# A two-layer backbone on one core: layer 0's first projection unit by quarters, and a re-ordered expert route before its mixture of experts

## The chip, the core and the metric

The kernel runs on one core of one Trainium2 chip. Its time is the device time of one execution in microseconds. The core's engines are TensorE (PE, matrix products), VectorE (DVE), ScalarE (ACT), GpSimd (POOL) and SyncE (SP, which here issues nearly all loads). Each engine works through its own instructions in order; one engine waits for another, or for a transfer, by semaphores.

## What is computed

Two layers over 256 latent tokens and, in layer 0, also 256 context tokens of width 1024, all in fp32. Layer 0's mixer is a gated recurrence (RG-LRU) beside a gated linear attention (GLA), layer 1's is a grouped-query attention. Each is followed by a mixture of 16 experts in 4 groups, of which every token takes two experts of one group. Cut to what matters here:

```python
def adaln(cvec, w, b):                       # shift, scale and gate of both sub-layers
    m = jax.nn.silu(cvec) @ w + b
    return tuple(m.reshape(m.shape[0], 6, 1, D_MODEL)[:, j] for j in range(6))

hl = modulate(rmsnorm(xl, norm1[i]), sh1l, sc1l)      # h * (1 + scale) + shift, per column
hc = modulate(rmsnorm(xc, norm1[i]), sh1c, sc1c)
# layer 0: project(h) = split(h @ w_in), its first 512 columns are xa; u = dwconv(xa)
xl = xl + g1l * yl
hl2 = modulate(rmsnorm(xl, norm2[i]), sh2l, sc2l)

def hier_moe(h, wg, bg, we, be, w1, w3, w2):
    p_group = softmax(t @ wg + bg);  w_group, g_idx = top_k(p_group, 1)
    e_val, e_idx = top_k(logits of the experts in that group, 2)
    w_exp = softmax(e_val) * w_group
    for e in range(16):
        he = silu(t @ w1[e]) * (t @ w3[e])
        out = out + comb[:, e:e + 1] * (he @ w2[e])
```

## The kernel before

**Weights.** About 305 MB come from HBM through one queue, SP's, in a fixed list (`order`, with `plan`). `feed(key)` hands out the next weight tile and lets `pump` issue loads as far ahead as there are slots; a slot is a 1 MB tile `raw`, and a load into it waits until the last reader of what lay there is done. `less_slots` and `more_slots` take slots out and put them in. Where full precision is wanted, a weight half (128x1024) is split by `split` (L534) into `whi`, a rounded copy made on ACT, and `wlo`, the rest, made on DVE or POOL; the moved operand is split in the same way (`hhi`, `hlo`, or `xh`, `xl`), and `mm3` (L557) adds three products hi·lo, hi·hi and lo·hi.

**Order.** A scheduler places most instructions by their dependences and priorities. `pin(where)` (L156) switches single engines to the order of the program, by the table `PIN`: letters a, d, g, p, s for ACT, DVE, POOL, PE and SP.

**The first unit** (layer 0). The norm's scale and shift come from a product of the conditioning vector with `w_ada`. For the first norm it is made in four parts: `ad0(n, h)` (L448) loads 4 chunks of 256 KB for each half of part n, multiplies them, and `ad0_cols` (L460) copies the result (ACT, `ad`), turns it on PE, and makes columns `A` (scale) and `B` (shift) of two 128-blocks of channels on DVE. `norm_T` (L620) turns the normed input to `xw` (channels on partitions); `finish(n)` scales and shifts two of its eight blocks (4 DVE instructions of 128x256) and splits them into `hhi` (ACT) and `hlo` (DVE). `first_unit` (L680) multiplies by the first 512 columns of `w_in`: 8 blocks x 4 column groups x 3 products = 96 matmuls into four accumulators, block after block; a table `AD0` says after which of its 16 steps the next `ad0` half or `finish` is written. `LO_U0` puts its four `wlo` on POOL. Of the other loads, `mod[0]` (0.25 MB) comes ahead of these weights, `bd` and `mod[1]` behind the third part. The `lam` instructions are a chain of some twenty tiny DVE instructions on the recurrence's parameters, free to fall between.

**From there to the route** PE works through the other units of `w_in`, the recurrence, the linear attention and `w_out`.

**Layer 0's route** (L798 to L1060). For each of four token tiles, `choose` (L813) takes the two best experts from the logits, with masks `Mb`, `Mf` and per choice `M`. `tile_` (L885) writes the normed tokens `h2x` to DRAM; for the last tile it does so on ACT and POOL (`on_pool`). `route_end` (L920) finds each token's place within its expert by a product of `Mb` with a triangle `tri`, ranks the experts by their counts (`units`, L967), and sorts them into 12 units: the four largest experts have a unit each, and the others share one by two. `prepare` and `tables` (L1010, L1045) make one-hot matrices `oh` of the places and multiply them with the tokens' numbers: the lists `t0i`, by which POOL's indirect DMAs gather each unit's tokens `xg` from DRAM. `prep_x` (L1570) turns and splits these (`xh`, `xl`), and `hidden(i, n, h)` (L1614) multiplies them with half h of weight n of unit i. Which expert a unit has is read from `order` by SP (L1545) before its loads can be issued. At L1666 all engines read a count and at L1667 branch around a block for tokens beyond their expert's room. Three loads are issued ahead of this branch, on slots opened by `more_slots` with a small POOL copy each (`state["behind"]`).

**The rest** is layer 0's experts, layer 1's attention, its route (with a branch at L2174) and its experts in 8 pairs.

Nearly every instruction goes through one helper, L144, so the profile's groups are told apart by tile names.

## Time and profile before

| | |
|---|---|
| three runs | 1022.48, 1022.91, 1026.24 us, median 1022.91 |
| the profiled execution | 1020.54 us, span from first to last instruction 1018.8 us |
| granted TensorE clock, mean | 0.956 of full |
| busy, share of the span | PE 90%, DVE 52%, ACT 39%, POOL 16% |
| moved by DMA | 304.56 MB, 299 GB/s in the mean |

The stages in the profiled execution, in us from its start: 0 to 72 the first unit, to 300 the rest of the mixer, 300 to 345 the route with the branch, to about 580 the steady part of layer 0's experts, to about 640 their end, to 780 layer 1's attention, to 800 its route, and to 1019 its experts. The mean busy shares hide these differences, so the windows by stage are read first, then the timeline inside the two stages that the change touches. PE's busy time counts a matmul from its start to a modelled end, and two in a row overlap; the distance from one start to the next is the better measure.

### The profile page before, as it was taken

To read this page: it belongs to the slowest core of one execution; us is meant where nothing else is said; L and a number is where in the kernel's file an instruction comes from. 1 tells how busy PE (TensorE), PEld (TensorE's weight loads), DVE (VectorE), ACT (ScalarE), POOL (GpSimd) and SP (SyncE) were. 2 spreads that over 40 slices of the span, in tenths; PEclk is the share of its full clock that TensorE was granted. 3 is DMA by queue.
4 is the path that set the end of the run, shared out by engine and by line. 5 is a ranking of instruction groups with operands and counts; after the bars stand their busy time and mean duration, and the time that the engine had idled before them with its cause. 6 is when DMAs were issued, how large, how long until landed. Compare 5 with 4: busy or idle time off the path is not lost. (4 is left out here: it accounts for less than half of the span.)

```text
span 1018.8 us, 12604 instructions
## 1 busy us (share of the span) xinstructions
PE 913.9 (90%) x4549; PEld 535.3 (53%) x4549; DVE 534.8 (52%) x1039; ACT 396.2 (39%) x687; POOL 162.5 (16%) x163
## 2 busy tenths in 40 slices
PE   5899997999991899989999966998996899999997
PEld 3456465667761555647466433774575444443432
DVE  5458578538587565636456347878657111111112
ACT  3236745144231544637455423453545222121210
POOL 2103332040503400001100233023001000000000
PEclk9899999999995899999999978999998999999999
DMA  9925454559541899999999976845928699999993
GB/s 315 384 100 218 155 198 172 206 182 336 197 160 49 307 419 421 421 420 403 408 422 400 380 306 248 302 171 200 369 95 307 234 419 417 416 418 414 417 414 136
DMA packets 63165, 304.56 MB, mean 299 GB/s; under 512 B 8578, under 2 KB 17666, under 8 KB 35056
## 3 DMA queue, kind: packets, MB, share of 16 engines
q1 hardware_dynamic: 55216, 284.56, 71.4%
q0 software_dynamic: 5120, 14.06, 3.7%
q10 hardware_dynamic: 2752, 4.98, 1.3%
q8 instruction: 40, 0.66, 0.3%
q14 instruction: 37, 0.30, 0.1%
HBM read 294.76 MB, written 12.58 MB: 302 GB/s over the span
## 5 line engine op out<-in xcount | busy, mean ns | idle before, releaser
L144 DVE TENSOR_TENSOR wlo<-raw,whi 128x1024 fp32r<-128x1024 f32 x138 | 170.4, 1250 | 77.4 <-ACT whi L144 70.2
L144 ACT ACTIVATE whi<-raw 128x1024 fp32r<-128x1024 f32 x140 | 146.4, 1057 | 119.4 <-PE acc L144 100.4
L144 PE MATMUL aux<-raw,x 128*64 128x512 f32 x488 | 116.3, 597 | 2.0 <-PEq L2174 1.4
L144 PEld LDWEIGHTS aux<-raw,x 128*64 128x64 f32 x488 | 34.5, 136 | 62.9 <-issue 58.6
L144 PE MATMUL acc<-raw,xf 128*64 128x512 f32 x256 | 62.3, 598 | 2.2 <-DMA raw<-in_w_dram 2.2
L144 PE MATMUL aux<-raw,sl 128*64 128x512 f32 x240 | 58.7, 610 | 0.7 <-ACT sl L144 0.7
L144 PE MATMUL acc<-wlo,xh 128*128 128x512 f32 x128 | 52.1, 407 | 6.4 <-DVE wlo L144 3.6
L144 PE MATMUL ada<-raw,cT 128*32 128x512 f32 x320 | 54.7, 616 | 1.0 <-DMA raw<-in_w_ada_dram 1.0
L144 PE MATMUL acc<-whi,xh 128*128 128x512 f32 x128 | 53.5, 418 | 0.0
L144 PE MATMUL acc<-whi,xl 128*128 128x512 f32 x128 | 51.8, 405 | 0.0
L144 PE MATMUL acc<-raw,hf 128*64 128x512 f32 x128 | 38.6, 659 | 7.9 <-DMA raw<-in_w_dram 7.8
L144 DVE SCALAR_TENSOR_TENSOR aux<-aux,ws,mod 128x512 f32<-128x512 f32 x8 | 6.1, 760 | 73.3 <-PE aux L144 73.3
L144 PE MATMUL acc<-hhi,whi 128*128 128x512 f32 x96 | 38.5, 417 | 6.2 <-ACT hhi L144 6.2
L144 POOL DMA_INDIRECT yd<-y,t0i x10 | 11.7, 1173 | 191.6 <-ACT y L144 156.5
L144 PE MATMUL acc<-whi,h 128*128 128x512 f32 x128 | 41.7, 400 | 0.0
L144 PEld LDWEIGHTS acc<-raw,xf 128*64 128x64 f32 x256 | 19.1, 136 | 38.4 <-issue 30.9
L144 PE MATMUL acc<-hlo,whi 128*128 128x512 f32 x96 | 38.9, 406 | 0.2 <-DVE hlo L144 0.2
L144 PE MATMUL acc<-hhi,wlo 128*128 128x512 f32 x96 | 39.0, 406 | 0.0
L144 DVE TENSOR_TENSOR he<-sl,aux 128x512 f32<-128x512 f32 x8 | 8.4, 1056 | 56.2 <-PE aux L144 56.2
L144 PEld LDWEIGHTS aux<-raw,sl 128*64 128x64 f32 x240 | 18.2, 140 | 37.1 <-issue 35.0
L144 PEld LDWEIGHTS acc<-wlo,xh 128*128 128x128 f32 x128 | 25.1, 196 | 12.3 <-DVE wlo L144 4.0
L144 PEld LDWEIGHTS acc<-whi,xh 128*128 128x128 f32 x128 | 25.0, 195 | 10.1 <-issue 3.5
(444 smaller groups left out, 1850.5 us busy)
## 6 DMA issues: line engine op xcount, KB each, us to landing
raw<-in_w_dram SPq DMA_DIRECT2D x151, 1024.0 KB, 15.0
raw<-in_w_ada_dram SPq DMA_DIRECT2D x38, 1024.0 KB, 6.3
raw<-in_w_dram SPq DMA_DIRECT2D x72, 512.0 KB, 11.5
raw<-in_w_in_dram SPq DMA_DIRECT2D x10, 1024.0 KB, 5.1
raw<-in_w_ada_dram SPq DMA_DIRECT2D x32, 256.0 KB, 6.9
raw<-in_w_qkv_dram SPq DMA_DIRECT2D x6, 1024.0 KB, 12.8
xres<-in_w_dram SPq DMA_DIRECT2D x5, 1024.0 KB
raw<-in_w_out_dram SPq DMA_DIRECT2D x4, 1024.0 KB, 7.5
```

What stands on the lines that cost most here:

```text
L144: ins = f(*a, **k)
```

## The change

**The first unit.** It is written as a pipeline over four quarters of two blocks each: 8 products hi·hi, then the next part's `ad0` with its copy, 8 products with `hlo`, the turn of the copy and the columns, 8 products with `wlo`, then the next part's scaling and splitting. Program order is kept on PE, ACT and DVE throughout. The four `wlo` are on DVE. The `lam` chain is ahead of the norm. The loads of `mod[0]` and `mod[1]` come together with `bd` behind the third quarter; `pcol` and the input come first.

**Layer 0's route.** The last tile's `h2x` is made on DVE, with its second half behind the choice (`early`). The masks per choice (`MM`) are made tile by tile in `choose`. `to_units` makes the eight one-hot matrices in two DVE instructions and one PE batch; the order of the experts (`experts`), the weights, counts (`others`, `weights_of`) and the hold list come behind the gathers. The first two gathers write into one tile, `xg01`, that ACT zeroes early. One load is issued ahead of the branch, and the branch stands ahead of `prep_x(0)` and all weight splits of unit 0; the slots of `parts_p` are opened behind `prep_x(1)`, without POOL's copies. Layer 1's route takes the shorter `weights` too.

```diff
-PIN = dict(pair='p', px='g', m0='p')
+PIN = dict(pair='p', px='padg', re='da', tb='dag', m0='p', n1='pad', xa='pad')
-LO_U0 = '1111'
@@ loads
-    sp.dma_start(mod[0], I["bada"][0])
...
-            if n == 3:
-                sp.dma_start(bd, I["bd"])
-                sp.dma_start(mod[1], I["bada"][1])
@@ first_unit
-        for n in range(4):
-            if n % 2 == 0:
-                raw = feed(("w_in", 0, n // 2))
-            state["lo"] = pool if LO_U0[n] == "1" else dve
-            wh, wl = split(raw[:, n % 2 * 1024:(n % 2 + 1) * 1024])
...
-                    mm3(pss[m], w, (hh[:, k, :], hl[:, k, :]), k == 0, k == KD - 1)
...
-                while at and at[0] == 4 * n + m:
-                    at.pop(0)
-                    todo.pop(0)()
+        copy, turn, rest = columns(0)
+        copy()
+        turn_last()
+        turn()
+        scaled(6)
+        rest()
+        x, hi = weights_hi(0)
+        modulate(0)
+        w = hi, weights_lo(x, hi)
+        scaled(7)
+        for n in range(3):
+            products(n, 0, w)
+            for h in range(2):
+                ad0(n + 1, h)
+            copy, turn, rest = columns(n + 1)
+            copy()
+            x, hi = weights_hi(n + 1)
+            products(n, 1, w)
+            turn()
+            rest()
+            products(n, 2, w)
+            modulate(n + 1)
+            w = hi, weights_lo(x, hi)
+        sp.dma_start(bd, I["bd"])
+        for l in range(2):
+            sp.dma_start(mod[l], I["bada"][l])
+        for m in range(4):
+            for kk in range(2):
+                for j in range(3):
+                    product(3, m, kk, j, w)
+            done(m, pss[m])
@@ tile_
-                if on_pool:
-                    act.activation(a, x[:, n * 512:(n + 1) * 512], AF.Copy, scale=rss[t])
-                    pool.tensor_tensor(a, a, A2[i][n], op=ALU.mult)
...
+                if late and n:
+                    todo.append(shift)
                 else:
...
+                    shift()
@@ to_units (new)
+            def one_hot(k):
+                sl = slice(k * NT, (k + 1) * NT)
+                dve.tensor_tensor(oh[:, sl, :], iota.unsqueeze(1).to_broadcast([P, NT, P]),
+                                  pk[:, sl].unsqueeze(2).to_broadcast([P, NT, P]), op=ALU.is_equal)
...
+            for n in range(NK):
+                pe.matmul(ps[:, 0:2 * NU], oh[:, n, :], v[:, n, 0:2, :].rearrange("p a u -> p (a u)"),
+                          start=(n == 0), stop=(n == NK - 1))
@@ from the gathers to the first expert
+    xg01 = parts_p.tile([P, 2048], F32, tag="raw", name="xg01")
+    act.activation(xg01.rearrange("p (n s) -> p n s", s=P), iota.unsqueeze(1).to_broadcast([P, 16, P]), AF.Copy, scale=0.0)
...
+    for e in range(2):
+        fetch_x(e)
+    R.experts()
...
+    state["behind"] = None
+    pump(state["fed"] + 1 + len(slots))
+    more_slots(raw2_p, N_RAW2 - R_ST - R_YB)
+    R.others()
+    wgt = weights_of()
...
-    pin("px")
-    for e in range(2):
-        with high_if(FH):
-            fetch_x(e)
-    xgs0 = xgs[0]
-    prep_x(0)
-    prep_x(1)
-
-    state["behind"] = (wgt[:, 0:1], xgs0[:, 0:1], xs[0][0][:, 0, 0:1].bitcast(F32), ident[:, 0:1])[BEH]
-    more_slots(raw2_p, N_RAW2 - R_ST - R_YB)
-    more_slots(parts_p, N_PARTS)
     rv = nc.values_load(R.cnt[0:1, 0:1], min_val=0, max_val=NTOK)
     with tc.If(rv > 0):
...
+    pin("px")
+    prep_x(0)
+    pin("tb")
+    ahead()
+    pin("px")
+    prep_x(1)
+    more_slots(parts_p, N_PARTS)
     pin("m0")
     hidden(0, 0, 0)
```

How this moves instructions, at four places. PE in the first unit, from the turn of part 0 on, before (`ad` is a part of the norm's product, `acc` the unit's accumulators):

```order
L144 MATMUL aux<-ident,ad_307 128x128 x4
L144 MATMUL ad_343<-raw,cT 32x512 x3
L144 MATMUL acc<-hhi,whi 128x512 x3
L144 MATMUL ad_343<-raw,cT 32x512
L144 MATMUL acc<-hlo,whi 128x512
L144 MATMUL acc<-hhi,wlo 128x512
```

The same place after:

```order
L136 MATMUL aux<-ident,ad_301 128x128 x4
L136 MATMUL acc<-hhi,whi 128x512 x8
L136 MATMUL ad_340<-raw,cT 32x512 x8
L136 MATMUL acc<-hlo,whi 128x512 x8
L136 MATMUL aux<-ident,ad_349 128x128 x4
L136 MATMUL acc<-hhi,wlo 128x512 x8
```

The first quarter's 8 products hi·hi stand ahead of the next part's product, and that part's copy is turned before the quarter's last 8 products; before, part 1 was turned after all 24. On DVE, the last part and the unit's end, before:

```order
L144 TENSOR_REDUCE v_472<-aux 128x8
L144 TENSOR_TENSOR A_0_136<-v_472,n1c 128x4
L144 TENSOR_TENSOR B_0_137<-v_472,b1c 128x4
L144 TENSOR_TENSOR A_0_136<-A_0_136,bn 128x4
L144 TENSOR_SCALAR xw<-xw,A_0_136,B_0_137 128x256 x4
L144 TENSOR_TENSOR hlo<-xw,hhi 128x512
L144 TENSOR_TENSOR wlo<-raw,whi 128x1024 x2
```

and after:

```order
L136 TENSOR_REDUCE v_475<-aux 128x8
L136 TENSOR_TENSOR A_0_173<-v_475,n1c 128x4
L136 TENSOR_TENSOR B_0_174<-v_475,b1c 128x4
L136 TENSOR_TENSOR A_0_173<-A_0_173,bn 128x4
L136 TENSOR_SCALAR xw<-xw,A_0_173,B_0_174 128x256 x4
L136 TENSOR_TENSOR hlo<-xw,hhi 128x512 x2
L136 TENSOR_TENSOR wlo<-raw,whi 128x1024 x3
```

The first of the three `wlo` is now the quarter's own, which was POOL's; the other two belong to the next unit in both. On POOL, the end of the route before (`h2x` is the last tile, `xg` the gathered tokens, L1666 the count):

```order
L144 TENSOR_TENSOR xa_2424<-xa_2424,row 128x512
L144 TENSOR_TENSOR h2x<-xa_2424,row 128x64x8
L144 TENSOR_TENSOR xa_2428<-xa_2428,row 128x512
L144 TENSOR_TENSOR h2x<-xa_2428,row 128x64x8
L144 MEMSET xg 128x1024
L144 COPY raw<-ident 128x1
L144 DMA xg<-h2d_112,t0i 128x1024
L144 MEMSET xg 128x1024
L144 DMA xg<-h2d_112,t0i 128x1024
L144 COPY raw<-ident 128x1 x3
L1666 TENSOR_LOAD cnti
```

and after:

```order
L136 TENSOR_TENSOR r_2222<-ssq,half_neg 128x1
L136 TENSOR_TENSOR r_2305<-ssq,half_neg 128x1
L136 TENSOR_TENSOR r_2386<-ssq,half_neg 128x1
L136 DMA xg_2528<-h2d_113,ix 128x1024 x2
L1781 TENSOR_LOAD cnti
```

Nothing but the two gathers is left of it. On ACT, around the branch before (L1666 and L1667):

```order
L144 ACTIVATE whi<-raw 128x1024 x2
L144 ACTIVATE m_2473<-m_2473 128x4
L144 ACTIVATE whi<-raw 128x1024 x2
L144 ACTIVATE xh<-aux 128x512 x2
L144 ACTIVATE xf<-aux 128x512 x2
L144 ACTIVATE whi<-raw 128x1024 x2
L1666 TENSOR_LOAD cnti
L1667 COMPARE_AND_BRANCH
```

and after, behind the branch's end:

```order
L1782 UNCONDITIONAL_BRANCH
L136 ACT_TABLE_LOAD
L136 ACTIVATE xh<-aux 128x512 x2
L136 ACTIVATE whi<-raw 128x1024 x4
L136 ACTIVATE xf<-aux 128x512 x2
L136 ACTIVATE whi<-raw 128x1024 x4
```

All eight copies `whi` of unit 0, of which six stood ahead of the branch, now follow it.

## Rows read from the trace of the kernel before

**Rows 1.** Windows by stage: length, busy per engine (instructions), TensorE clock, DMA share, GB/s.

```profile
80.00:300.00 220.00, 210.27 (x1297) 138.46 (x1295) 151.84 (x254) 96.58 (x162) 60.94 (x62) 0.99 0.56 202
...
320.00:345.00 25.00, 13.19 (x52) 10.90 (x53) 10.21 (x38) 6.03 (x8) 4.11 (x7) 0.64 0.45 165
346.00:580.00 234.00, 227.44 (x1004) 137.79 (x1004) 129.13 (x142) 126.63 (x155) 31.31 (x34) 0.99 1.00 408
```

**Rows 2.** Timeline, first unit: start, length, engine, line, operation, count, idle before and releaser.

```profile
17.90 0.60 ACT L144 ACTIVATE ad<-ad 128x512 f32<-128x512 f32 x1 [2.27 <-PE ad L144]
...
20.49 4.65 POOL L144 TENSOR_TENSOR wlo<-raw,whi 128x1024 fp32r<-128x1024 f32 x2 [7.30 <-ACT whi L144]
20.60 2.27 DVE L144 TENSOR_SCALAR lam<-lam 128x8 f32<-128x8 f32 x1
...
27.03 1.22 PE L144 MATMUL acc<-hhi,whi 128*128 128x512 f32 x2 [4.34 <-ACT hhi L144]
```

**Rows 3.** SP timeline, part 3 issued; DMA view of 20 to 60 us, median landing.

```profile
26.88 7.78 SPq L144 DMA_DIRECT2D raw<-in_w_ada_dram  x8
...
raw<-in_w_ada_dram SPq DMA_DIRECT2D x16, 256.0 KB, 7.3
```

**Rows 4.** Windows inside the first unit, columns as in the first group.

```profile
30.00:33.00 3.00, 3.00 (x7) 2.07 (x7) 0.00 (x0) 0.00 (x0) 0.00 (x0) 0.51 1.04 402
33.00:36.00 3.00, 3.00 (x14) 2.46 (x14) 0.00 (x0) 0.00 (x0) 0.00 (x0) 1.00 1.07 348
...
50.00:52.00 2.00, 0.57 (x2) 0.25 (x2) 1.95 (x6) 1.26 (x2) 0.00 (x0) 1.00 0.73 240
```

**Rows 5.** Timeline, second part, and the end of the first unit.

```profile
36.61 1.06 PE L144 MATMUL ad<-raw,cT 128*32 128x512 f32 x8
...
37.82 0.60 ACT L144 ACTIVATE ad<-ad 128x512 f32<-128x512 f32 x1 [10.05 <-PE ad L144]
...
38.48 0.66 PE L144 MATMUL aux<-ident,ad 128*128 128x128 f32 x4 [0.80 <-ACT ad L144]
...
39.79 1.38 DVE L144 TENSOR_SCALAR xw<-xw,A,B 128x256 f32<-128x256 f32 x4
...
40.56 1.28 ACT L144 ACTIVATE hhi<-xw 128x512 fp32r<-128x512 f32 x2 [2.14 <-DVE xw L144]
...
63.31 2.36 DVE L144 TENSOR_TENSOR wlo<-raw,whi 128x1024 fp32r<-128x1024 f32 x2 [0.26 <-ACT whi L144]
...
68.02 2.06 ACT L144 ACTIVATE xa<-acc 128x512 f32<-128x512 f32 x4 [3.27 <-PE acc L144]
```

**Rows 6.** Timeline, the route from the last tile to the first transposed tokens.

```profile
306.38 1.32 POOL L144 TENSOR_TENSOR h2x<-xa,row 128x512 f32<-128x512 f32 x1
...
306.49 1.31 DVE L144 TENSOR_TENSOR gt<-lg 128x80 f32<-128x80 f32 x1
...
319.22 1.22 DVE L144 TENSOR_TENSOR wlo<-raw,whi 128x1024 fp32r<-128x1024 f32 x1
...
323.57 3.70 PE L144 MATMUL aux<-vals,oh 128*128 128x36 f32 x14 [1.12 <-DVE vals L144]
...
328.79 1.25 POOL L144 DMA_INDIRECT xg<-h2d,t0i  x1 [8.31 <-DVE t0i L144]
...
333.39 1.94 PE L144 MATMUL aux<-ident,xg 128*128 128x128 f32 x8 [6.11 <-DMA xg<-h2d,t0i]
```

**Rows 7.** Timeline around layer 0's branch, then PE behind layer 1's.

```profile
343.50 0.70 PE L144 MATMUL acc<-wlo,xh 128*128 128x512 f32 x1 [2.77 <-PEq L1667]
...
345.40 8.76 SPq L144 DMA_DIRECT2D raw<-in_w_dram  x4
...
352.25 0.39 PE L144 MATMUL acc<-whi,xl 128*128 128x512 f32 x1
...
796.45 3.65 PE L144 MATMUL aux<-raw,x 128*64 128x512 f32 x16 [1.36 <-PEq L2174]
```

**Rows 8.** Window behind layer 0's branch, columns as in the first group.

```profile
342.00:346.00 4.00, 2.50 (x6) 2.07 (x7) 1.23 (x1) 1.56 (x2) 0.73 (x1) 0.70 0.18 68
```

358 lines of the change are left out of this document (208 added, 150 removed).

## The prediction

> **What bounds the kernel now.** I read the windows by stage first [rows 1]. From 80 to 300 us PE is busy 210.3 of 220 us at a clock of 0.99: PE sets the pace there, and whatever comes before moves the whole stretch with it. From 346 to 580 us PE is busy 227.4 of 234 us while the DMA share is 1.00: the loads set the pace, closely followed by PE. Between them, from 320 to 345 us, PE is busy 13.2 of 25 us at a clock of 0.64 and DMA 0.45: a chain of waits, and nothing is the bound by its size. The first 72 us are another such chain.
>
> In the first unit, the timeline shows why [rows 2]. Part 0's copy `ad` is at 17.90, yet the first product starts at 27.03, after PE had waited 4.34 us for `hhi`. In between POOL makes two `wlo` (4.65 us), and a `lam` instruction of 128x8 elements on DVE takes 2.27 us beside it. The second part shows the undisturbed length [rows 5]: copy at 37.82, turn at 38.48, scaling from 39.79, `hhi` from 40.56, which ends for its first block at about 41.2. That is 3.4 us against 9.1. The copies `xa` that end the unit start at 68.02, so it is over at about 69. Its last inputs had come long before: the last chunk of part 3 is issued at 34.7 and the median landing is 7.3 us later, so 42 [rows 3]. From 42 to 69 the unit works off what it could have done while the loads came.
>
> **The first unit, after.** A quarter's chain, in the order of PE's program, with lengths from [rows 4, 5]. Fourteen matmuls fit in 3.00 us at full clock, so one takes 0.22 us, against seven, 0.43 us, at half clock.
> - 8 products hi·hi: 1.8.
> - 16 matmuls of the next part (two batches of 8 at 1.06): 2.1.
> - 8 products with `hlo`: 1.8; the copy (0.60) lies beside them.
> - turn 0.66, columns about 0.7 (from the turn's end to 39.79), one block's scaling 0.7 (half of 1.38), one `hhi` 0.64 (half of 1.28).
>
> This is 8.4 us; the 8 products with `wlo` (1.8) lie beside the columns and the scaling. The quarter's own `wlo` on DVE (half of 2.36, so 1.2) comes after the scaling and is wanted two batches later, so it is hidden, except in the last quarter.
>
> The first quarter starts at 17.9 + 3.4 = 21.3; 0.7 us earlier, since 0.25 MB (`mod[0]`) at 348 GB/s are no longer ahead of it; and up to 1.5 us later, since three blocks' turns and scalings by row stand ahead of the columns on DVE. I take 22.0. Three chains lead to 22.0 + 25.2 = 47.2. The last quarter multiplies column group by column group and wants `wlo` at once: that is there after the second `hhi`, an `hlo` (half as wide as a split: estimated 0.7) and the split, 0.6 + 0.7 + 1.2, at 49.7; some 22 products remain, 4.8, and a few of the next work's matmuls, 0.5. The end is 55, against 69: **14 us less**. The loads allow it: part 3 lands at about 41.3, and the third quarter wants it at 22.0 + 16.8 + 1.8 = 40.6, under one us of wait. `bd` and `mod`, now behind the third quarter, find the queue empty.
>
> The bounds: 15 if the start is at 21.3; 11 if the first quarter's PE work (6.4 us in the chain) runs mostly at half clock. Behind it the stretch to 300 us has the same order of instructions on every engine, apart from a few `hf` and `u` on DVE, so the 14 us pass through; DVE is busy only 152 of 220 us there [rows 1].
>
> **Layer 0's route, up to the gathers.** Three covers go away. POOL's work on the last tile: while it makes `h2x` (1.32), a small comparison on DVE takes 1.31 [rows 6]; four such POOL instructions lie beside the choice of the last tile, and I take 2 us for them. Three `wlo` stand in the chain of the lists on DVE, 1.22 each: 3.7. The one-hot products take 3.70 us for the last 14 matmuls of 16; eight remain, about 2, so 1.7 less, but the two large one-hot instructions and the masks per tile cost some of it. Together 7 us: the first gather starts at about 322 in the time of before, not at 328.8.
>
> **And behind them.** Here most of it is given back. Ahead of the first product now stand eight weight matmuls and the branch on PE, and behind the branch ACT makes the table load, `xh`, and all eight `whi`, each followed by its `wlo`. My estimate is that the tokens and the counts are there near 327, and that the weight matmuls, at half clock, bring PE to the branch at about 331.5. The branch kept PE idle for 2.77 us in layer 0, and in layer 1, with little DMA traffic, for 1.36 [rows 7]; I take 2.8, so 334.3. Then the turns of the first half of the tokens (1 of 1.94 at half clock, [rows 6]), two `xh` (I estimate 0.6 each, as for `hhi`), and a `whi` of about 1.1 and a `wlo` of 1.22 with what lies between: the first product is at about 338.4, some 3 us later than before. No branch interrupts it now, but eight `wlo` at 1.22 take 9.8 us, and the first products run at half clock: unit 0's 48 products end at 351 to 352.5. In the kernel before the last of them starts at 352.25 [rows 7]. So for PE the gain is nil to 1 us.
>
> For the stage that follows, the loads count [rows 1]. Before, 3 MB were issued ahead of the branch, and behind it DMA moved 68 GB/s for 4 us, [rows 8]; the next load is issued at 345.40 [rows 7]. After, only 1 MB is issued ahead of it: 2 MB less, some 5 us at 408 GB/s. Against that, loads resume near 333, as slots come free by the splits, and three gathers of 0.5 MB each, which ran between the loads, now run while the queue is short: 3.7 us. The 4 us of near silence are gone for the greater part. I take **2 us less** in all, with bounds of 7 less (the whole lead is kept) and 4 more (the slots come free so late that the missing 2 MB are paid and little else is gained).
>
> A rule of the Trainium skill bears on the price of the branch. Runtime: NRT & Kernel Launch, Instruction fetch mechanics, says that a taken branch out of the fetched window forces a DMA fetch of the target before the engine can go on. The two branches agree with it, 2.77 against 1.36 us of idle PE with and without loads in the queues. By it the branch after, with 1 MB queued and not 3, would be nearer to 1.4, and the sum 1 us lower.
>
> **Layer 1's route** computes its weights with fewer instructions, but PE is busy with its gather products up to the branch: 0, within 0.5 either way.
>
> **The sum.** The profiled execution took 1020.5 us (span 1018.8), 2.4 below the median of the three runs, 1022.9. From the median: 1022.9 - 14 - 2 = **1006.9**.
>
> **Rivals.**
> - *The route keeps its lead.* If slots come free as fast as the splits run, the loads stand 7 us earlier, and PE follows. That gives 1022.9 - 14 - 7 = 1002, and 1000 with the better bound of the first unit. For it speaks that the silence behind the branch shrinks; against it, that all of unit 0's splits stand behind the branch. Chance 0.20.
> - *The early loads do not do what they say.* One load is ahead of the branch where there were three. If unit 0's last slots come free only near 347, and the two new slots of `parts_p` wait behind them in SP's order, the stream is 4 us later: 1022.9 - 14 + 4 = 1013. Chance 0.17.
> - *The first unit is bound by DVE or waits, not by the chain above.* The splits and columns are all on one engine now, in program order; if each quarter loses 2 us by that, or one quarter runs at half clock (see below), only half of the 14 is won: 1022.9 - 7 - 2 = 1014, up to 1017. Chance 0.09.
> - *Slower: the clock stays down in the first unit.* PE's clock fell to one half after it had waited 4.34 us ahead of its first product, and came back within some 6 us of work [rows 2, 4]; in the window from 50 to 52 us, with PE busy 0.57 of 2 us, it stayed at full. The pipeline has waits of 1 to 2 us before every quarter. If the clock were at one half throughout, a quarter would cost 24 x 0.43 + 16 x 0.26 + 1.3 for the turn = 15.8 and not 8.4, four of them 63: the end at 22 + 63 = 85, 16 us later than now, and the time 1022.9 + 16 - 2 = 1037. Two such quarters use up the 14 us, and from three on the kernel is slower. The row from 50 to 52 speaks against it. Chance 0.03.
>
> The skill has a rule that points that way: TensorE: Matmul & The Clock Gate, Part 1, calls the throttled state the default, which activity releases. By it alone a unit cut into short batches with waits would run at half clock, and the time would be the 1037 of the last rival; the row from 50 to 52 us, full clock across such a wait, does not bear this out.
>
> **How the numbers follow.** The sum as forecast, 0.51. Its own bounds are 1022.9 - 15 - 4 = 1004 and 1022.9 - 12 - 0 = 1011. The range goes to 999 at the low side (first rival with the better bound, less 1) and 1014 at the high one (second rival, and the start of the third). What is left out, the third and the last rival and the ends of the others, is under 0.2. A measurement of this kernel can tell about 0.5%, 5 us, from no change: faster by more (under 1017.8) has 0.93, within it 0.04, slower 0.03.
>
> **What would show it.** Right: the first product near 22, quarters about 8.4 us apart, `xa` near 54, clock 1.00 from 25 us on, and the stretch behind 14 us earlier; the first gather 20 to 21 us earlier than before, the last product of unit 0 only 14 to 15; the DMA share at 1.00 some 16 us earlier. Wrong: quarters over 10 us apart, PE idle for `wlo` or `hlo`, clock 0.5 inside the unit; or unit 0 finishing more than 4 us earlier or later, in its own frame, than before.

## The result, and the profile after

The changed kernel takes **1011.12 us** in the median (1013.40, 1007.97, 1008.94 and 1013.31), the kernel before 1023.49 in four executions beside it (1022.48 to 1026.24). The ratio is 0.9873, with an interval from 0.9833 to 0.9912: faster by 0.9 to 1.7%. The forecast was 1006.9 with a range from 999 to 1014. The profiled execution is the slowest of the four, 1013.40 us with a span of 1011.7; before it was 1020.54 with 1018.8. All lines in this kernel are L136, and the branch is L1781 and L1782.

The windows by stage of the changed kernel (length, busy time of each engine with its instructions, granted TensorE clock, DMA share, GB/s) answer to [rows 1, 4]:

```profile
16.00:20.00 4.00, 4.00 (x19) 0.72 (x17) 3.67 (x7) 0.00 (x0) 0.00 (x0) 0.50 1.00 376
20.00:24.00 4.00, 1.89 (x13) 1.47 (x9) 2.02 (x9) 2.28 (x4) 0.00 (x0) 0.81 1.10 348
24.00:28.00 4.00, 3.85 (x12) 2.26 (x16) 2.99 (x4) 0.53 (x1) 0.00 (x0) 0.61 1.09 347
...
40.00:60.00 20.00, 19.36 (x91) 11.95 (x90) 13.77 (x29) 8.31 (x12) 0.00 (x0) 1.00 0.94 353
60.00:72.00 12.00, 11.01 (x38) 6.74 (x37) 11.86 (x18) 7.76 (x12) 2.53 (x2) 1.00 0.26 97
...
306.00:331.00 25.00, 10.12 (x46) 9.83 (x47) 11.38 (x54) 3.26 (x6) 5.07 (x5) 0.50 0.39 135
```

Two things are to be seen. From 40 to 60 us PE is busy 19.36 of 20 us, where the kernel before had it waiting (0.57 of 2 us in [rows 4]). And from 16 to 20 us, and through most of 24 to 28, PE runs at the lower of its two levels, 1.2 in place of 2.4 GHz (half clock from here on), in the very place where the first quarter lies. The timeline of the first unit answers to [rows 2, 5]:

```profile
16.46 3.64 PE L136 MATMUL ad<-raw,cT 128*32 128x512 f32 x16
20.25 0.60 ACT L136 ACTIVATE ad<-ad 128x512 f32<-128x512 f32 x1 [4.89 <-PE ad L136]
...
23.93 0.49 PE L136 MATMUL acc<-hhi,whi 128*128 128x512 f32 x1 [2.11 <-ACT hhi L136]
24.58 3.09 PE L136 MATMUL acc<-hhi,whi 128*128 128x512 f32 x7 [0.15 <-ACT hhi L136]
...
34.47 2.54 PE L136 MATMUL acc<-hhi,whi 128*128 128x512 f32 x8 [0.24 <-ACT hhi L136]
...
43.48 0.49 PE L136 MATMUL acc<-hhi,whi 128*128 128x512 f32 x1 [0.24 <-ACT hhi L136]
44.12 1.90 PE L136 MATMUL acc<-hhi,whi 128*128 128x512 f32 x7 [0.15 <-ACT hhi L136]
...
45.95 1.92 PE L136 MATMUL ad<-raw,cT 128*32 128x512 f32 x16
...
47.80 2.13 PE L136 MATMUL acc<-hlo,whi 128*128 128x512 f32 x8
...
49.77 0.60 PE L136 MATMUL aux<-ident,ad 128*128 128x128 f32 x4
...
60.74 0.60 ACT L136 ACTIVATE xa<-acc 128x512 f32<-128x512 f32 x1 [0.80 <-PE acc L136]
```

The quarters start at 23.93, 34.47, 43.48 and 52.49: 10.5, 9.0 and 9.0 us long. The last `xa` starts at 60.74. In [rows 5] the copies of before start at 68.02. By same-named instructions of both traces, start to start (the middle of the differences within 20 us), the changed kernel is 8.2 us ahead from 110 to 215 us. Then 3 us are lost within 10 us, which the section on the experiments comes to; 4.6 us of lead arrive at the route.

The route of the changed kernel, in a timeline that answers to [rows 6, 7]:

```profile
293.99 0.39 PE L136 MATMUL acc<-whi,mlo 128*128 128x512 f32 x1
...
311.35 3.61 PE L136 MATMUL aux<-vals,oh 128*128 128x24 f32 x16 [5.99 <-DVE vals L136]
...
316.56 1.25 POOL L136 DMA_INDIRECT xg<-h2d,ix  x1 [18.93 <-DVE aux L136]
...
320.27 3.59 PE L136 MATMUL aux<-vals,oh 128*128 128x12 f32 x16 [5.31 <-DVE vals L136]
...
328.07 3.65 PE L136 MATMUL aux<-ident,xg 128*128 128x128 f32 x16 [4.21 <-DVEq L1782]
331.64 0.71 PE L136 MATMUL acc<-whi,xh 128*128 128x512 f32 x1
...
343.78 0.39 PE L136 MATMUL acc<-whi,xl 128*128 128x512 f32 x1
```

The first line is the last product of `w_out`; in the trace of before it starts at 298.07, so 4.1 us later. All of the route is best read in the time of before, by adding 4.1:

| | forecast | measured + 4.1 | before |
|---|---|---|---|
| first gather | 322 | 320.7 | 328.79 [rows 6] |
| PE at the branch | 331.5 | 328.0 (320.27 + 3.59 + 4.1) | |
| PE goes on behind it | 334.3 | 332.2 | 343.50 [rows 7] |
| first product | 338.4 | 335.7 | 335.16 |
| last product of unit 0 | 351 to 352.5 | 347.9 | 352.25 [rows 7] |

The 335.16 of before is the first product's start in its trace. PE finishes unit 0 some 4 us earlier in the route's own time, where nil to 1 had been forecast. Of this, at 400 us the lead is 7.9 us, at 460 us 5.1 and at 800 us 5.4: behind the route the loads take most of it back, as forecast, and about 1 us stays in this trace.

### The profile page after: what moved, and what is told of

It reads as the page before. It is cut to its first block, busy times and chain, and to the rows that moved or that the text cites. A ratio compares the mean times of both kernels' runs of the same rounds, so it can differ in the third digit from the quotient of the medians.

```text
span 1011.7 us, 12591 instructions
## 1 busy us (share of the span) xinstructions
PE 912.4 (90%) x4565; PEld 539.5 (53%) x4565; DVE 534.9 (53%) x1031; ACT 397.0 (39%) x686; POOL 144.3 (14%) x147
## 5 line engine op out<-in xcount | busy, mean ns | idle before, releaser
L136 DVE TENSOR_TENSOR wlo<-raw,whi 128x1024 fp32r<-128x1024 f32 x142 | 173.0, 1237 | 71.8 <-ACT whi L136 69.6
L136 ACT ACTIVATE whi<-raw 128x1024 fp32r<-128x1024 f32 x140 | 146.1, 1058 | 116.6 <-PE acc L136 103.8
L136 PE MATMUL aux<-raw,x 128*64 128x512 f32 x488 | 116.3, 597 | 1.5 <-PEq L2294 0.8
L136 PEld LDWEIGHTS aux<-raw,x 128*64 128x64 f32 x488 | 34.5, 136 | 62.5 <-issue 56.7
L136 PE MATMUL acc<-raw,xf 128*64 128x512 f32 x256 | 63.0, 599 | 3.5 <-DMA raw<-in_w_dram 3.5
L136 PE MATMUL aux<-raw,sl 128*64 128x512 f32 x240 | 57.0, 594 | 0.7 <-ACT sl L136 0.7
L136 PE MATMUL ada<-raw,cT 128*32 128x512 f32 x320 | 55.0, 618 | 1.7 <-DMA raw<-in_w_ada_dram 1.7
L136 PE MATMUL acc<-wlo,xh 128*128 128x512 f32 x128 | 51.0, 398 | 6.1 <-DVE wlo L136 6.1
L136 PE MATMUL acc<-whi,xh 128*128 128x512 f32 x128 | 52.7, 412 | 0.0
L136 PE MATMUL acc<-whi,xl 128*128 128x512 f32 x128 | 50.6, 395 | 0.0
L136 PE MATMUL acc<-raw,hf 128*64 128x512 f32 x128 | 37.2, 628 | 7.7 <-DMA raw<-in_w_dram 7.6
L136 DVE SCALAR_TENSOR_TENSOR aux<-aux,ws,mod 128x512 f32<-128x512 f32 x8 | 6.1, 758 | 71.6 <-PE aux L136 71.6
L136 PE MATMUL acc<-whi,h 128*128 128x512 f32 x128 | 41.9, 402 | 0.0
L136 PE MATMUL acc<-hhi,whi 128*128 128x512 f32 x96 | 38.2, 430 | 3.3 <-ACT hhi L136 2.9
L136 PEld LDWEIGHTS acc<-raw,xf 128*64 128x64 f32 x256 | 19.1, 136 | 40.3 <-issue 30.6
L136 POOL DMA_INDIRECT yd<-y,ix x10 | 11.7, 1174 | 201.7 <-ACT y L136 185.4
L136 DVE TENSOR_TENSOR he<-sl,aux 128x512 f32<-128x512 f32 x8 | 8.5, 1059 | 56.2 <-PE aux L136 56.2
L136 PEld LDWEIGHTS aux<-raw,sl 128*64 128x64 f32 x240 | 17.8, 137 | 35.8 <-issue 33.7
L136 PE MATMUL acc<-hlo,whi 128*128 128x512 f32 x96 | 35.9, 409 | 0.0
L136 PE MATMUL acc<-hhi,wlo 128*128 128x512 f32 x96 | 35.0, 400 | 0.0
L136 PEld LDWEIGHTS acc<-wlo,xh 128*128 128x128 f32 x128 | 24.5, 191 | 12.2 <-DVE wlo L136 7.3
L136 PEld LDWEIGHTS acc<-whi,xh 128*128 128x128 f32 x128 | 24.4, 191 | 10.1 <-issue 3.5
```

The lines of the kernel that those rows point to most:

```text
L136: ins = f(*a, **k)
```

## The experiments

All times are medians. The kernel before took 1022.9 to 1023.8 in each group of runs. A lead is the middle of the start-to-start differences of same-named instructions against the profiled execution of before; at 120 us it shows the first unit, from 280 to 800 us the route and what follows. That execution of before (1020.54) is 2.4 to 3.3 us below those medians, so a lead runs short of a difference of medians by about that much, and no trace shows in which stage.

### The same kernel once more

No edit.

> The changed kernel once more, for the spread of its runs and a second profile. In the first profile PE's clock was at one half from 14 to 30 us and again from 208 to 216 us, and the stretch behind lost 3 us at the second place though the instructions and the wait before it are those of the kernel before. Theory A (these half-clock spells differ from run to run and are the difference between 1008 and 1013): another profile has other spells; an execution near 1008 has one of them fewer or shorter, its first unit ends near 58 and not 61 us, or it does not lose 3 us near 208. Theory B (the spells belong to the new order): every execution has them, and 1008 against 1013 comes from elsewhere.

Measured: 1009.07 (1007.61, 1009.35, 1014.36, 1008.80), ratio 0.9879 [0.9848, 0.9910]. So the same program spreads over 6 us again, and the mean granted clock goes with it: 0.961, 0.962, 0.953 and 0.960 in this order; 0.956, 0.964, 0.963 and 0.958 in the first four. The profile is of the 1007.61 execution. Its first product starts at 21.70, which is the forecast's 22.0; from 12 to 20 us its clock is whole, and then it has its own half-clock spell in the first quarter. In its windows, with the columns as above:

```profile
16.00:20.00 4.00, 2.96 (x24) 1.10 (x16) 3.75 (x9) 1.66 (x2) 0.00 (x0) 1.00 1.02 372
20.00:24.00 4.00, 2.15 (x5) 1.51 (x6) 3.91 (x10) 1.26 (x2) 0.00 (x0) 0.82 1.10 349
24.00:28.00 4.00, 4.00 (x22) 1.52 (x21) 0.75 (x2) 0.23 (x1) 0.00 (x0) 0.75 1.09 346
```

The lead is 10.4 us at 120 us, and still 10.4 at 220. So the 3 us that the first trace lost near 210 are not of the change's making. What happened there is in the windows from 206 to 218 us, first of the profiled execution above, then of this one:

```profile
208.00:210.00 2.00, 1.54 (x14) 1.10 (x15) 2.00 (x2) 0.00 (x0) 0.40 (x1) 0.81 0.17 70
210.00:216.00 6.00, 6.00 (x60) 4.59 (x59) 0.62 (x1) 0.00 (x0) 0.86 (x1) 0.50 0.57 190
```

```profile
208.00:210.00 2.00, 2.00 (x39) 1.54 (x36) 0.34 (x1) 0.00 (x0) 0.13 (x1) 1.00 0.89 213
210.00:216.00 6.00, 6.00 (x44) 4.11 (x43) 0.17 (x1) 3.42 (x18) 3.60 (x5) 1.00 0.93 330
```

In both, PE had waited 1.1 us for POOL's `at` just before (until 208.46 and 206.18), as in the trace of before (until 216.59, there too with no fall of the clock). In one execution six us of work at half clock follow, in the other two none. The same wait, 1.11 to 1.14 us, stands in all fourteen profiles of this case: in four of them half clock follows (the profile of the result and, below, those of the route's added products, of the first unit's and of the route alone, the last two more briefly), in ten it does not. The spell in the first quarter is another matter: it is in both profiles here, and the section on added products comes back to it.

### The two halves of the change, each alone

The first unit alone, on the kernel before:

```diff
-PIN = dict(pair='p', px='g', m0='p')
+PIN = dict(pair='p', px='g', m0='p', n1='pad', xa='pad')
...
-    hT, finish_hT = norm_T(hp, wide, bd)
+    hT, finish_hT = norm_T(hp, wide)
...
-    def first_unit(hT, finish, done):
+    def first_unit(hT, parts, done):
```

> The kernel before with the new first unit alone, old route. Theory A (the first unit gives 8 to 14 us by its clock, the route 2): 1023 minus 10 = about 1013, 1009 to 1015. Rival (the route gives most of the 12 us, the first unit's gain being absorbed before the route): 1018 to 1022.

Measured: 1013.58, ratio 0.9902 [0.9877, 0.9926]. First product at 23.13, lead 8.4 at 120 us, 7.8 at 280, 7.5 at 800: what the first unit gains passes through to the end, but it is about 10 us by the times, not 14.

The route alone, on the kernel before:

```diff
-PIN = dict(pair='p', px='g', m0='p')
+PIN = dict(pair='p', px='padg', re='da', tb='dag', m0='p')
...
+            one_hot(0)
...
+            one_hot(1)
...
-    pin("px")
-    prep_x(0)
-    prep_x(1)
     more_slots(raw2_p, N_RAW2 - R_ST - R_YB)
-    more_slots(parts_p, N_PARTS)
...
+    pin("px")
+    prep_x(0)
+    pin("tb")
+    ahead()
+    pin("px")
+    prep_x(1)
+    more_slots(parts_p, N_PARTS)
```

> The kernel before with the new route alone, old first unit. Theory A: PE is 5 to 6 us earlier at the end of unit 0, but the load stream only 2 us, and the time is 1023 minus 2 = 1021, 1018 to 1023. Rival: the route gives 6 us or more, 1014 to 1017.

Measured: 1019.40 in seven executions, ratio 0.9960 [0.9946, 0.9974], so 2.7 to 5.5 us. Its profiled execution was its slowest, 1025.33, and lost 5 us between 217 and 263 us, ahead of the route: some 3.5 in two spells of half clock and 1.5 in two waits of PE for DVE; from 280 to 800 us its lead changes by +1.2. The same stretch gives +0.9 in the first trace of the whole change, +1.3 in its repeat, and -0.3 with the first unit alone. The two halves add up: 1023.2 - 9.6 - 3.8 = 1009.8, against 1009.1 for both in the same group.

### PE kept at work in the first unit

Nineteen small products, whose result nothing uses, in PE's two waits ahead of the first product:

```diff
+        for _ in range(9):
+            pe.matmul(ps[:, 0:P], ident, ident, start=True, stop=True)
...
         turn()
+        for _ in range(10):
+            pe.matmul(pss[3][:, 0:P], ident, ident, start=True, stop=True)
```

> The changed kernel with 9 matmuls of the identity, written over later, in PE's wait for the norm (near 12 us) and 10 in its wait for the first hhi (near 22 us). Theory A (the late start and the long first quarter of the profile, 10.5 us against 9.0 for the next two, come from the half clock): clock 1.00 from 12 us on, first product near 22, quarters of 9.0, unit over near 57, time 1007 to 1009 with less spread. Rival (the start waits for DVE and the loads): first product stays near 24, time unchanged near 1011.

Measured: 1009.36, ratio 0.9859 [0.9840, 0.9878]. The clock is 1.00 in every window of the first unit, the first quarter takes 9.5 us (22.30 to 31.80). Yet the lead at 120 us is 10.7, only 0.3 over the repeat's 10.4. The timeline shows why:

```profile
11.62 2.55 PE L136 MATMUL aux<-ident 128*128 128x128 f32 x18
...
14.01 1.06 PE L136 MATMUL aux<-ident,rs 128*128 128x128 f32 x8
```

The turn of `rs`, for which ACT and then DVE wait, stands behind the added products and starts at 14.01, in the repeat at 13.31. The first product of the unit comes 0.6 us later than there (22.30 against 21.70), and that takes back more than half of the 1.0 us that the first quarter gains. The quarter is still 9.5 and not 9.0, with 0.38 us of it a wait for the load of the next part. Twelve profiles have the new first unit: in the three with added products the clock is 1.00 in every window of 4 us from 8 to 32 us, in the nine without them it lies between 0.50 and 0.80 from 24 to 28 us. So half clock in the first quarter belongs to the program and is no accident of an execution. The spells of half clock elsewhere remain (2 us are lost by 280 in this profile), and the median stays.

### The first unit's `wlo` on POOL again

```diff
-            dve.tensor_tensor(y, x, hi.bitcast(F32), op=ALU.subtract)
+            pool.tensor_tensor(y, x, hi.bitcast(F32), op=ALU.subtract)
```

> The changed kernel with the four wlo of the first unit on POOL, as before, pipeline and orders kept. Theory A (the 4.65 us of POOL beside DVE's small instructions were a large part of the old start and would be again): DVE instructions of 2 us beside them, quarters of 10 to 11 us in place of 9, time 4 to 6 us more, about 1015. Theory B (the pipeline hides them, since wlo is wanted two batches later): quarters near 9, within 2 us of 1010.

Measured: 1020.35, ratio 0.9967 [0.9951, 0.9983]. This one line is worth 9 to 11 us by the medians, nearly all of the first unit's gain, and the lead at 120 us is gone (-0.8). The timeline, of POOL and DVE, then of PE:

```profile
22.10 2.34 POOL L136 TENSOR_TENSOR wlo<-raw,whi 128x1024 fp32r<-128x1024 f32 x1 [9.25 <-ACT whi L136]
22.13 2.33 DVE L136 TENSOR_TENSOR B<-v,b1c 128x4 f32<-128x4 f32 x1
...
33.60 2.38 POOL L136 TENSOR_TENSOR wlo<-raw,whi 128x1024 fp32r<-128x1024 f32 x1 [9.17 <-ACT whi L136]
34.38 0.19 DVE L136 TENSOR_REDUCE v<-aux 128x8 f32<-128x32 f32 x1 [6.43 <-PE aux L136]
34.60 1.40 DVE L136 TENSOR_TENSOR A<-v,n1c 128x4 f32<-128x4 f32 x1
```

```profile
26.02 3.97 PE L136 MATMUL acc<-hhi,whi 128*128 128x512 f32 x8 [4.23 <-ACT hhi L136]
...
37.69 0.49 PE L136 MATMUL acc<-hhi,whi 128*128 128x512 f32 x1 [1.48 <-ACT hhi L136]
...
47.95 0.50 PE L136 MATMUL acc<-hhi,whi 128*128 128x512 f32 x1 [1.49 <-ACT hhi L136]
```

An instruction on 128x4 elements, otherwise 0.15 us, ends on DVE only when POOL's `wlo` beside it does. It stands in the columns, ahead of the scaling and `hhi`, so PE waits 4.2 us ahead of the first quarter, 1.5 ahead of the second and third, and 2.8 ahead of the last; the second quarter takes 10.3 us, the third 12.5. It is the pairing of [rows 2] and [rows 6], now once per quarter.

### The branch: away, late, and with a second load ahead of it

Without the branch and its block, this kernel leaves out the work for tokens beyond their expert's room:

```diff
-    rv = nc.values_load(R.cnt[0:1, 0:1], min_val=0, max_val=NTOK)
-    with tc.If(rv > 0):
...
-            with tc.For_i(0, NE, 1) as e:
-                spare(0, wk, d4, e, jx, jw, 1)
```

> The changed kernel without layer 0's branch and the block behind it for tokens beyond their expert's room (left out). It measures the branch itself. In the changed kernel's profile PE waits 4.2 us for it, and the loads pause from 324 to 327 us. Theory A (from here on the loads set the pace, and they lose only their pause): 3 to 4 us less than the changed kernel, about 1006. Theory B (PE's chain counts): 5 to 6 us less, about 1004. Theory C (the branch is hidden, since loads wait for slots in any case): within 1 us of 1010.

Measured: 1012.52, ratio 0.9902 [0.9866, 0.9938]: no gain in the times. In its trace the lead grows by 2.8 us from 280 to 800, against 1.3 in the repeat, so the branch is worth some 1.5 us where it now stands, if one pair of traces is enough to tell. PE's wait becomes one for the gathered tokens (1.31 us), and the next loads wait for slots that the splits free.

The branch behind the tokens' preparation and the splits, where it was before:

```diff
+    pin("px")
+    prep_x(0)
+    pin("tb")
+    ahead()
+    pin("px")
+    prep_x(1)
+    more_slots(parts_p, N_PARTS)
     rv = nc.values_load(R.cnt[0:1, 0:1], min_val=0, max_val=NTOK)
...
-    pin("px")
-    prep_x(0)
-    pin("tb")
-    ahead()
-    pin("px")
-    prep_x(1)
-    more_slots(parts_p, N_PARTS)
```

> The changed kernel with the branch back behind the turned tokens, the weight splits and the opened slots, as it stood before. Theory A (the early branch is part of the route's gain, since the splits then run while loads are issued without a break): 2 to 3 us more, about 1013. Theory B (its place is of no account, the shorter chain to the gathers does it all): within 1 us of 1010. Theory C (splits ahead of the branch hide it, as I priced it in the prediction): 2 us less, about 1008.

Measured: 1018.37, ratio 0.9955 [0.9936, 0.9974], 7 to 9 us slower than the changed kernel. Its trace is 0.7 us ahead of the repeat's at the last product of unit 0 (337.67 against 338.34), 16 us behind where unit 2's tokens are turned (365.44 against 349.32), and 8.4 behind from 440 us on, of which 1.8 came from ahead of the route. Its timeline, and one window against the same window of the repeat (the second):

```profile
348.35 1.12 PE L136 MATMUL aux<-ident,he 128*128 128x128 f32 x4 [6.71 <-DVE he L136]
...
350.19 0.95 POOL L136 MEMSET xg<- 128x1024 f32 x1 [34.80 <-SPq L1789]
...
365.44 0.90 PE L136 MATMUL aux<-ident,xg 128*128 128x128 f32 x3 [8.18 <-DMA xg<-h2d,ix]
```

```profile
340.00:355.00 15.00, 8.29 (x32) 3.02 (x28) 2.14 (x3) 3.08 (x4) 0.95 (x1) 0.77 0.88 357
```

```profile
340.00:355.00 15.00, 15.00 (x72) 8.13 (x70) 9.47 (x12) 7.88 (x11) 0.00 (x0) 1.00 0.94 375
```

POOL stands at the branch for 34.80 us, by the trace's account for SP's sequencer, and in SP's order the loads that wait for the splits' slots are now ahead of the branch. Two things follow. ACT, too, stands at the branch (its next instruction comes at 345.34, after 6.19 us), so the values `he` that it and DVE make for PE are late, and PE waits 6.71 us for them: that is the window above, in which PE is busy 8.29 of 15 us. And the later units' gathers are behind the branch on POOL, so PE then waits 8.18 us for tokens. So it is not the branch's own few us that the early place saves, but what queues behind it.

A second early load, by one of the later slots:

```diff
     more_slots(raw2_p, N_RAW2 - R_ST - R_YB)
+    more_slots(parts_p, 1)
     R.others()
...
-    more_slots(parts_p, N_PARTS)
+    more_slots(parts_p, N_PARTS - 1)
```

> The changed kernel with a second load ahead of the branch, into the free one of the two tiles of parts_p, whose slot is opened earlier. Theory A (the load stream sets the stage's pace and lost by having one load ahead where there were three): 1 MB earlier is 2.5 us, time 2 to 2.5 us less, about 1008. Theory B (the stream is soon held by slots that the splits free, whatever lies ahead): within 1 us of 1010; or 1 us more, if SP comes to the branch later.

Measured: 1011.33, ratio 0.9883 [0.9842, 0.9925]. From 280 to 800 us its lead grows by 1.9, the repeat's by 1.3; the times don't tell them apart. Whether one load or two stand ahead of the branch doesn't show. That fits Theory B: from 312 to 368 us of the repeat, SP's queue waits 24.8 us in all for `wlo`, the splits that free slots.

### Shorter quarters, extra work in the route, and all together

The products block by block, with the turn after four of the eight `hlo` products:

```diff
+        def products(n, j, w, kks=(0, 1)):
+            for kk in kks:
+                for m in range(4):
...
-            products(n, 1, w)
+            products(n, 1, w, (0,))
             turn()
+            products(n, 1, w, (1,))
             rest()
```

> The changed kernel with two edits inside a quarter: the eight products of each kind go block by block, so that four run before the second hhi is wanted, and the turn of the next part stands after four of the hlo products, not after eight. Theory A (the quarter of 9.0 us, priced at 8.4, is PE's chain: the wait for the second hhi is its 0.6 us, and 0.9 us of products need not stand ahead of the turn): quarters of about 8, first unit 3 us shorter, time 1006 to 1008. Rival (the quarters are paced by the landing of the next part or by DVE): quarters stay at 9, time unchanged near 1010.

Measured: 1010.76, ratio 0.9883 [0.9856, 0.9910]. The quarters do shrink to 8.1 us (33.95, 42.07, 50.15), but the time doesn't move: this profile has its first product at 24.37 with the clock at 0.50 from 16 to 20 us, and PE waits 2.05 us for `wlo` near 53.9. The edit has two parts, and the last experiment's third quarter parts them: by blocks, but with the turn at its old place, it takes 8.5 us (39.61 to 48.09).

Thirty-four unused products in PE's two waits of the route, whose order is then the program's (`tb='padg'`):

```diff
+            for _ in range(16):
+                pe.matmul(ps[:, 0:P], R.MM.rearrange("p k t e -> p (k t e)"), ident, start=True, stop=True)
...
+                for _ in range(18):
+                    pe.matmul(ps[:, 0:P], R.MM.rearrange("p k t e -> p (k t e)"), ident, start=True, stop=True)
```

> The changed kernel with 16 extra products ahead of the one-hot batch and 18 ahead of the weight batch, written over later, with PE in program order there. Theory A (the half clock costs each batch of 3.6 us its half, and all of the chain to the first product follows): both batches about 1.9 us, the first gather 1.7 us earlier and the branch 3.4 us earlier in the kernel's own frame, the time 1 to 3 us less, since slots come free by the splits. Rival (the stage is paced by loads that wait for slots, and the clock there is of no account): batches shorter but the time within 1 us of 1010.

Measured: 1010.37, ratio 0.9876 [0.9853, 0.9898], one of the changed kernel's own values. The two batches do fall to 1.9 us each, and the first gather comes 1.6 us earlier than in the changed kernel when each is counted from the same place ahead of the route. But unit 0 ends only 0.6 us earlier, and the lead grows by 1.6 from 280 to 800 us, as it does without the edit (0.9 and 1.3). The rival holds.

All three together (eight products, not ten, in the second wait of the first unit):

```diff
+            products(n, 1, w, (0,))
             turn()
+            products(n, 1, w, (1,))
...
+        for _ in range(9):
...
+        for _ in range(8):
...
+            for _ in range(16):
...
+                for _ in range(18):
```

> The changed kernel with the block-by-block quarters, the extra products in the two waits at the start, and those of the route: the best version if the theories of these runs hold. First unit at full clock, over near 54; 1004 to 1006. If neither the quarters nor the clock can be bettered this way: 1009 to 1011.

Measured: 1007.85, ratio 0.9866 [0.9828, 0.9905]. The last quarter starts at 47.70, 2.5 us ahead of the repeat's 50.23, but at 120 us only 0.8 of that is left (11.25 against 10.42). DVE is busy 11.9 of 12 us behind the unit in this trace as in those of the changed kernel, so it is one suspect. The timeline of ACT, then of PE, shows another:

```profile
46.45 0.63 ACT L136 ACTIVATE hhi<-xw 128x512 fp32r<-128x512 f32 x1 [1.30 <-DVE xw L136]
46.99 1.99 ACT L136 ACTIVATE whi<-raw 128x1024 fp32r<-128x1024 f32 x2
48.88 0.61 ACT L136 ACTIVATE hhi<-xw 128x512 fp32r<-128x512 f32 x1
```

```profile
51.41 0.50 PE L136 MATMUL acc<-hhi,wlo 128*128 128x512 f32 x1 [2.05 <-DVE wlo L136]
...
68.97 1.04 PE L136 MATMUL ada<-raw,cT 128*32 128x512 f32 x2
```

The scheduler had put two splits of the next unit between the two `hhi` of the last quarter. The second `hhi`, its `hlo` and the `wlo` behind it came 1.8 us late, and PE waited 2.05 us. The first quarter, 9.7 us at full clock, held something too: PE's weight loads waited 1.35 us for the load of part 1 (26.22). The last kernel tests the order on ACT. It is the one of all three additions, with the turn ahead of the last quarter back behind all eight products, which puts the two `hhi` next to each other again:

```diff
             products(n, 1, w, (0,))
-            turn()
+            if n < 2:
+                turn()
             products(n, 1, w, (1,))
+            if n == 2:
+                turn()
             rest()
```

> The three additions together (products by blocks, extra matrix products in the waits of the first unit and of the route), with one difference: ahead of the last quarter the turn of the modulation stands behind all eight hlo products again, as in the changed kernel. In the three-addition kernel two splits of the next unit's weights (1.99 us of ACT at 46.99) stood between the two hhi of the last quarter, the hlo and the wlo behind them came 1.8 us late (wlo at 50.14), and PE waited 2.05 us for wlo at 51.41; here the built order has both hhi next to each other again. Theory A (this order on ACT gave back what the shorter quarters had won): the wait of 2.05 for wlo falls under 0.5, the later turn costs 0.6, and from 120 to 290 us the same instructions come 1.2 to 1.6 us earlier than in the three-addition kernel, so 2.0 to 2.4 earlier than in the repeat of the changed kernel where both run at full clock; median 1005 to 1007.5. Theory B (VectorE, busy in 11.9 of 12 us behind the first unit, is the limit there whatever comes ahead): the wait goes over to u (1.25 us at 65.69 grows past 2), and from 120 on the lead on the three-addition kernel is under 0.5; median 1007 to 1009. A spell of half clock ahead of 60 us would hide 1 to 3 us of either and is read from the granted clock first.

Measured: **1006.04** (1005.04 to 1011.20, five executions), ratio 0.9841 [0.9815, 0.9867]: below both kernels, and 3 to 5 us under the changed kernel's two medians, though its interval still touches theirs. The `hhi` of the last quarter in ACT's timeline, and the starts of three quarters and of the longest wait up to 70 us in PE's:

```profile
47.41 1.28 ACT L136 ACTIVATE hhi<-xw 128x512 fp32r<-128x512 f32 x2 [0.34 <-DVE xw L136]
```

```profile
31.49 2.03 PE L136 MATMUL acc<-hhi,whi 128*128 128x512 f32 x8
39.61 2.02 PE L136 MATMUL acc<-hhi,whi 128*128 128x512 f32 x8
48.09 0.49 PE L136 MATMUL acc<-hhi,whi 128*128 128x512 f32 x1 [0.24 <-ACT hhi L136]
64.93 1.96 PE L136 MATMUL aux<-u,bd 128*128 128x512 f32 x4 [1.00 <-DVE u L136]
```

The wait for `wlo` is gone and the one for `u` did not grow (1.00, as in the repeat). The lead at 120 us is 13.0, 1.74 over the kernel with the two splits in between. But not all of the 1.74 is the order on ACT. Of same-named instructions on PE, this kernel is ahead of the other by 0.50 us from 52 to 63 us, by 0.76 at `u` (64.93 against 65.69), and by 1.74 from the next `u` product on. DVE's timeline, the kernel with the splits first, then this one, and PE's where the last step comes:

```profile
50.14 3.49 DVE L136 TENSOR_TENSOR wlo<-raw,whi 128x1024 fp32r<-128x1024 f32 x3
```

```profile
49.33 3.49 DVE L136 TENSOR_TENSOR wlo<-raw,whi 128x1024 fp32r<-128x1024 f32 x3
```

```profile
68.22 1.96 PE L136 MATMUL aux<-u,bd 128*128 128x512 f32 x4
```

The order on ACT brings DVE's `wlo` 0.8 us earlier. From there DVE works without a gap past 75 us in both traces and hands the 0.76 on to `u`: it is the limit in that stretch, as Theory B had it, though neither of B's signs came. The other 0.98 us come from a second place. In the kernel with the splits the scheduler had put two of the eight products `ada` (68.97 above) ahead of the next `u` product, which then starts at 69.94; here, as in the changed kernel, all eight follow it. Two of them held PE about as long, 0.97 us, as all eight do together. So both parts are the scheduler's order, on ACT and on PE, and one edit changed both; no run parts them further.

## Why the prediction came out as it did

The direction, the place of the gain and the range held; the middle was 2 to 4 us too low, and two errors of opposite sign lie in it: 4 us too much for the first unit, about 2 too little for the route. That they half cancel is luck. Of the signs that the prediction named for being wrong, three came: a quarter over 10 us (the first), half clock inside the unit, and unit 0 ending 4.3 us earlier in its own frame.

**The first unit, -14 forecast, -10 measured** (first unit alone -9.6; lead 8.2 and 10.4 in the two traces). The steps:
- *The start, 22.0.* Right at full clock: 21.70 in the repeat, and 21.81, 22.17 and 22.30 with extra products. In the profiled execution 23.93, since the 16 matmuls ahead of it ran at half clock, 3.64 us where the repeat's took 1.92.
- *The quarter, 8.4.* Measured 9.0, by its own terms: first products 2.47 instead of 1.8, matmuls of the next part 1.86 (2.1), `hlo` products 1.97 (1.8), turn 0.63 (0.66), columns 0.62 (0.7), scaling 0.78 (0.7), `hhi` 0.68 (0.64). Nearly all of the difference is in the first term. The sum took one `hhi` as the start of eight products, but they go column group by column group over both blocks, so the second product wants the second `hhi`, 0.64 us later (43.48 and 44.12 above). Taken block by block, a quarter is 8.5, as priced; with the turn moved up as well, 8.1.
- *The first quarter* took 10.5 in both traces, with a spell of half clock in it: 1.5 us more than the others. The forecast had half clock there as a bound ("11 if ...") and full clock in its middle; all nine profiles without added products have it. And at full clock the quarter is still 9.5, 9.7 and 9.3 us in the three profiles with them: there PE's weight loads wait 0.38, 1.35 and 1.01 us for the load of part 1. The forecast had checked the landing of part 3 only.
- *The end, 55* became 60.7: 1.9 of it by the start, 3.3 by the three quarters, 0.5 by the last one.
- *That the gain passes through* held: 8.4 at 120 us and 7.5 at the end with the first unit alone; 10.4 and 11.2 in the repeat. The 3 us lost near 210 us belong to one execution.
- *The cover of DVE's own `wlo`*, costed at nothing, held: 1.22 us, and no quarter but the last waits for it.

In the repeat these add up: three times 0.6 for the second `hhi`, 1.5 for the first quarter, 0.5 for the last one, less 0.3 at the start, are 3.5 us of the 14, and its lead is 10.4. At full clock and by blocks the unit gives 13.0 (the last experiment, where the turn is earlier in two quarters, too), so the 14 was near the size of the program at full clock.

**The route, -2 forecast, about -4 measured** (2.7 to 5.5 by the route alone; 1 to 2 by the leads from 280 to 800 us). The first gather came 8.1 us earlier, forecast 7. Behind it all steps were forecast 2 to 5 us too late: the second product batch was done at 328.0 in the time of before, not at 331.5, and the first products ran at full clock from 332 us on, not at half. The branch cost more than forecast, 4.21 us of idle PE against 2.8. What bound the stage was named rightly: PE's lead of 7.9 us at 400 has fallen to 5.1 at 460, as the loads' pace sets in (in the repeat from 13.4 to 11.9). Between the 4 us of the times and the 1 to 2 of the leads, nothing shows where the rest lies. With 1 MB queued in place of 3 the idle at the branch was longer, not shorter. So what the prediction drew from the Trainium skill (Runtime: NRT & Kernel Launch, Instruction fetch mechanics), that fewer queued loads would bring it nearer to 1.4, did not come; the trace puts that wait down to DVE's sequencer, and no run here separates an engine's fetch from its waiting for the others.

**The rivals.** *The route keeps its lead* did not come: the lead falls back behind 400 us. *The early loads don't do what they say* falls too, and for a reason that it did not have: a second early load changes nothing that shows (1011.33). *Bound by DVE or waits* was half true: a quarter was 0.6 too long and the first at half clock, some 4 us instead of the 7 of that rival. *Slower by the clock* had the right mechanism at a small size: spells of 4 to 8 us at half clock, in the first quarter and near 210 us, but no quarter after the first in the two traces of the changed kernel, where PE's waits ahead of the second to fourth quarter are 0.24 us and not the 1 to 2 that the rival supposed. What stays open is why the spell near 210 us is in four profiles and not in the other ten.

## What to carry to other kernels

When a chain is cut into a pipeline, write a stage's instructions down with their operands in program order, and ask of each one which half of its input it wants: here 0.6 us per quarter hung on the second of eight products. Behind a branch at which all engines meet, the price is set by what each of them has queued ahead and behind it, not by the jump, so work that other engines wait for goes to the side where it can start. And before an engine's busy share is blamed for a gain that went missing, look for the one wait that took it: two splits that a scheduler had moved ahead made PE wait 2 us. Then follow the difference on to the end, instruction by instruction: putting them back gave 0.8 us, and another 1.0 came from an order on PE that changed with it.

## What the runs showed of the hardware

- Executions of one and the same program don't get the same clock. For the changed kernel, eight executions spread from 1007.6 to 1014.4 us with a mean clock from 0.964 to 0.953; for the last experiment 1005.04 at 0.972 and 1011.20 at 0.962. The same wait of PE of 1.1 us near 210 us is followed by half clock (some 4 to 7 us) in four profiles and by none in ten. Behind the wait of 2.1 us or more ahead of the first product, all nine profiles of the new first unit without added products have half clock (0.50 to 0.80 from 24 to 28 us).
- Nineteen products added in PE's waits held the clock at 1.00 through the first unit, and brought 0.3 us at 120 us: work that keeps the clock up delays what stands behind it, here by 0.7 us.
- Beside a 128x1024 subtraction on POOL (2.34 us), a 128x4 one on DVE took 2.33 and 1.40 us, alone 0.15. The reduction just ahead of the second of these, with one input and that from PSUM, kept its 0.19 us beside the same POOL instruction. The Trainium skill (SBUF — State Buffer, SBUF: two separate sides) has it so: one of the two engines holds the pair of ports that they share for a whole instruction, against DVE instructions with two inputs from SBUF or in a mode that uses both of DVE's ports; the trace agrees for two inputs, and the `lam` instruction of [rows 2], with one input and 2.27 us long, would be of the other kind, which no run here tests. Moving four such subtractions between the two engines moved the kernel by 9 to 11 us, though DVE was busy 25.0 and POOL 0 of the 40 us from 20 to 60 in the repeat, and 20.6 and 9.5 with the subtractions on POOL.
